# Gate and up of the second FFN, second half of the tokens: seven half-size products in place of eight

## The chip, the cores and the metric

The kernel runs on one core of one Trainium2 chip. The metric is the device time of one launch in microseconds; lower is better. All arithmetic is fp32: every factor of a matrix product is split into a high part of the type fp32r and the remainder, and a product is made of three matmuls (high by high, high by low, low by high).

## What is computed

One decoder layer for 1,024 prompt tokens and 64 sample tokens (1,088 in all, width 1,024). Around every sub-layer stands an RMSNorm before and one after:

```python
def swiglu(x, w_gu, w_down):
    gate, up = jnp.split(x @ w_gu, 2, axis=-1)
    return (jax.nn.silu(gate) * up) @ w_down

def macaron_half(x, g_pre, w_gu, w_down, g_post):
    return x + 0.5 * rmsnorm(swiglu(rmsnorm(x, g_pre), w_gu, w_down), g_post)
...
    hp = macaron_half(hp, ffn1_norm_pre[l], ffn1_w_gu[l], ffn1_w_down[l], ffn1_norm_post[l])
    ...
    hp = hp + rmsnorm(merge(fo, go, gg, gla_norm[l], w_out[l]), mix_norm_post[l])
    hp = macaron_half(hp, ffn2_norm_pre[l], ffn2_w_gu[l], ffn2_w_down[l], ffn2_norm_post[l])
```

Between the two FFNs lie attention and gated linear attention, which the change doesn't touch. The hidden width of an FFN is 2,752: 21 full blocks of 128 rows for gate and for up, and a tail of 64.

## The kernel before, in words

All activations lie transposed: 128 rows of the width on the partitions, tokens along the free axis. The second FFN runs twice, for tokens 0 to 511 (called f2 in the code, accumulator `p3.y`, in the trace and below `y0`) and for tokens 512 to 1,087 (called f3, 576 tokens, accumulator `p4.y`, the later `y1`). f3 is the last stage of the program. Its operand, the normed input of 576 tokens, lies split in `ub` (high and low); that of the first half lies in `ua`, which is free once f2 has made its last gate and up.

The hidden blocks are taken in groups: [0 (the tail), 1], [2 to 5], [6 to 9], [10 to 13], [14 to 17], [18, 19], [20, 21]. For a group, `job_gate` and `job_up` make gate and up of each block, and four jobs `job_down` then add the group's part of the down product to the accumulator. In f3 gate of one block is 24 matmuls on 256 tokens and 24 on 320 (eight blocks of the contraction by three), and up the same: 96 matmuls. ScalarE (ACT) takes Silu of gate out of PSUM, VectorE (DVE) multiplies it with up, and ACT and DVE split the result into `hh` and `hl`, the operands of the down product.

`Feed` brings the weights: a DMA of 512 KB into one of two buffers `wr`, a cast on ACT to `wh`, a subtraction on DVE to `wl`. There are three buffers each of `wh` and `wl`, so a weight is split only after the one three places earlier has been used up. The products go to three PSUM banks, `mm`; a bank is free when DVE or ACT has read it.

The program is written with a tile framework that tracks dependences by region and waits with semaphores. Each engine works through its own list strictly in order. The framework sorts these lists when it compiles, by its own model of what will be ready when, so an instruction can stand on an engine's list far from where the code issues it.

Of the kernel before, what the change touches and what calls it, by code (L numbers as in the profile page):

```python
# [8 lines left out]
F32 = mybir.dt.float32  # L9
# [23 lines left out]
NRAWW = 2  # L33
NCW = 320
# [31 lines left out]

class Feed:
# [7 lines left out]
    def _raw(self):  # L75
        s, nc = self.step, self.step.nc
        t = s.W.tile([P, KB * P], F32, name=s.uid("wr"), tag="wraw", bufs=NRAWW)
        pieces, _ = self.reqs[len(self.raws)]
        o = 0
        for p in pieces:  # L80
            n = p.shape[-1]
            nc.sync.dma_start(t[:, o:o + n], p)
            o += n
        self.raws.append((t, o))

    def _split(self):
# [5 lines left out]
        place = self.reqs[i][1]  # L92
# [8 lines left out]
    def pump(self, ahead=NW - 1):  # L101
        while len(self.parts) < min(len(self.reqs), self.freed + ahead):
            self._split()
        while len(self.raws) < min(len(self.reqs), len(self.parts) + NRAWW):
            self._raw()

# [6 lines left out]
    def free(self, n=1, ahead=NW - 1):  # L113
        self.freed += n
        self.pump(ahead)


class Step:
# [32 lines left out]
    def flush(self):  # L151
        while self.pend:
            self.pend.pop(0)()
# [142 lines left out]
    def norm(self, y, y0, c0, n, pool, post=None, pre=None, v=None, key=None):  # L296
# [24 lines left out]
        if post:  # L321
# [14 lines left out]
            if pre is None:  # L336
                return
# [17 lines left out]
    def ffn(self, w_gu, w_dn, f):  # L355
# [103 lines left out]
        def job_first(g, ws):  # L459
# [3 lines left out]
            for i, (c0, n) in enumerate(f.firsts):  # L463
                f.first(i)
                tail(ws[0], c0, n)
                if i == len(f.firsts) - 1:
                    self.feed.free(1, NW)
                gate(g[1], ws[1], c0, n)
# [12 lines left out]

        def job_down(g, d2, w, chunks, final):
            wt = None
            if HB_TAIL in g:
# [22 lines left out]
        for g, chunks, kind in f.plan:  # L507
# [5 lines left out]
            elif kind == "last":  # L513
# [4 lines left out]
                continue  # L518
            else:
# [9 lines left out]
    def work(self, jobs):  # L529
        self.feed = Feed(self, [r if isinstance(r, tuple) else (r, None) for rs, *_ in jobs for r in rs])  # L530
# [451 lines left out]


class Part:


    def __init__(self, **kw):
        self.__dict__.update(kw)


class StepB(StepA):
# [415 lines left out]
    def whole(self):  # L1407
# [122 lines left out]
        def mid4():  # L1530
# [5 lines left out]
        f2.after = lambda c0, n, v: self.norm(p3.y, 0, c0, n, p4.R, (5, self.h2, O["yT"]), None, v)  # L1536
# [8 lines left out]
                  plan=[(G[0], MID[1:], "first")] + [(g, MID[1:], "mid") for g in G[1:6]] + [(G[6], [(HALF, 320), (HALF + 320, 256)], "last")],  # L1545
                  place=lambda i: lambda: [u[:, 2 * i:2 * i + 2].rearrange("p a n -> p (a n)") for u in self.ua],
                  after=lambda c0, n, v: self.norm(p4.y, HALF, c0, n, p4.R, (5, self.h2, O["yT"]), None, v))

        f3.first = lambda i: self.need(("f2", CH[2 + i][0]))

        def start5():
            p4.close()
            f3.H, _ = self.pool("H2", keep=True)
        norm0 = self.norm(y, 0, *CH[0], F, pre=0, key="f1", v=[self.rms_quick(y, CH[0][1], F)])
# [100 lines left out]
```

## Time and profile before

| | |
|---|---|
| median of 3 runs | 2416.95 us (2416.03 to 2434.86) |
| profiled execution | 2429.76 us, of which 2428.0 us from its first to its last instruction |
| PE (TensorE) busy | 2346.4 us, 97% |
| DVE busy | 1174.9 us, 48% |
| ACT busy | 862.7 us, 36% |
| POOL (GpSimd) busy | 361.2 us, 15% |
| mean DMA rate | 136 GB/s |
| mean granted TensorE clock | 0.984 |

PE spans overlap: a matmul's record lasts longer than the distance to the next one, so the cost of a matmul is read from the distance of the starts. "PEld" is the weight load that goes beside the matmul before it. In f3 the trace has no POOL instruction from 2040 to 2340 us.

### The profile page before, as it was taken

The page shows a single profiled execution, that of the slowest core. Times are in us where ns is not written, and L with a number is a line of the kernel's source. Part 1 is how long each engine was busy: PE and PEld are TensorE (multiplying, and loading weights), DVE is VectorE, ACT ScalarE, POOL GpSimd, SP SyncE. Part 2 cuts the span into 40 slices and gives each one's busy share as a digit, 9 for nine tenths or more (in the row PEclk, how much of TensorE's full clock was granted, in tenths as well). Part 3 has the DMA queues.
Part 4 walks back from the last instruction along what each step waited for, and adds up shares of the span by engine and source line. Part 5 has one row for each costly group of instructions (what it writes and reads, how often), then busy time and mean ns, then how long its engine had stood idle before and what let it go on. Part 6 is the DMA issues. An engine that isn't in the chain of part 4 may idle for free.

```text
span 2428.0 us, 39284 instructions
## 1 busy us (share of the span) xinstructions
PE 2346.4 (97%) x15452; PEld 2074.3 (85%) x15452; DVE 1174.9 (48%) x2302; ACT 862.7 (36%) x1582; POOL 361.2 (15%) x420
## 2 busy tenths in 40 slices
PE   7999999999999999999998999999997999999997
PEld 6799999999989879899996656677787999999997
DVE  7223232232347774666464333358775774333345
ACT  5411111112134555755453222236455543222222
POOL 4000000000003230010134554611100320000002
PEclk9999999999999999999998999999998999999998
DMA  3111111111125476564357998755554534222222
GB/s 122 61 44 51 46 44 44 44 44 44 44 96 158 167 227 195 189 188 143 127 182 255 313 330 292 260 171 158 168 155 143 184 103 159 85 81 86 80 78 84
DMA packets 177082, 330.56 MB, mean 136 GB/s; under 512 B 25153, under 2 KB 100738, under 8 KB 176898
## 3 DMA queue, kind: packets, MB, share of 16 engines
q1 hardware_dynamic: 165234, 289.77, 36.8%
q0 software_dynamic: 11664, 38.28, 4.5%
q8 instruction: 122, 2.00, 0.3%
q14 instruction: 62, 0.51, 0.1%
HBM read 284.29 MB, written 43.69 MB: 135 GB/s over the span
## 4 chain that ended last, share of the span: by engine, by line
PE 76%; DVE 9%; DMA 4%; ACT 4%; issue 4%; POOL 2%; SPq 1%; POOLq 0%; DVEq 0%; ACTq 0%
PE mm L210 46%; PE mm L440 21%; PE po L878 2%; DVE wl L146 1%; PE sp L840 1%; DMA wr<-in_wout 1%; ACT wh L145 1%; PE tp L1073 1%; PE po L1088 1%; DVE qd L1177 1%; DVE fm L1060 1%; DVE pT L146 1%; PE pa L1218 1%; POOL y L328 1%; POOL ss L224 0%
## 5 line engine op out<-in xcount | busy, mean ns | idle before, releaser
L210 PE MATMUL mm<-ub,wh 128*128 128x320 f32 (+2 forms) x3776 | 774.9, 300 | 10.4 <-ACT ub L145 8.2
L210 PE MATMUL mm<-ua,wh 128*128 128x512 f32 (+2 forms) x2288 | 637.7, 365 | 2.2 <-ACT ua L351 1.4
L210 PEld LDWEIGHTS mm<-ub,wh 128*128 128x128 f32 (+1 forms) x3776 | 612.1, 190 | 19.4 <-ACT ub L145 8.4
L146 DVE TENSOR_TENSOR wl<-wr,wh 128x1024 fp32r<-128x1024 f32 (+1 forms) x294 | 356.5, 1213 | 448.3 <-ACT wh L145 445.3
L145 ACT CAST wh<-wr 128x1024 fp32r<-128x1024 f32 (+1 forms) x294 | 301.2, 1025 | 743.1 <-PE mm L210 314.7
L210 PE MATMUL mm<-ub,wl 128*128 128x320 f32 (+1 forms) x1872 | 556.1, 297 | 0.7 <-DVE wl L146 0.7
L210 PEld LDWEIGHTS mm<-ua,wh 128*128 128x128 f32 (+1 forms) x2288 | 401.2, 192 | 79.5 <-issue 23.9
L210 PE MATMUL mm<-ua,wl 128*128 128x512 f32 (+1 forms) x1136 | 406.3, 358 | 0.7 <-DVE wl L146 0.7
L210 PEld LDWEIGHTS mm<-ub,wl 128*128 128x128 f32 x1872 | 356.1, 190 | 0.9 <-DVE wl L146 0.9
L440 PE MATMUL mm<-hl,wh 128*128 128x256 f32 (+4 forms) x1088 | 353.1, 325 | 0.0
L440 PE MATMUL mm<-hh,wh 128*128 128x256 f32 (+2 forms) x1040 | 338.5, 326 | 1.4 <-DVE y L450 1.4
L440 PE MATMUL mm<-hh,wl 128*128 128x256 f32 (+2 forms) x1040 | 332.1, 320 | 0.0
L210 PEld LDWEIGHTS mm<-ua,wl 128*128 128x128 f32 x1136 | 217.2, 192 | 32.9 <-issue 1.6
L450 DVE TENSOR_TENSOR y<-y,mm 128x256 f32<-128x256 f32 (+2 forms) x272 | 130.3, 504 | 203.3 <-PE mm L440 202.9
L440 PEld LDWEIGHTS mm<-hl,wh 128*128 128x128 f32 (+1 forms) x1088 | 205.8, 189 | 21.1 <-issue 9.9
L224 POOL TENSOR_TENSOR ss<-ss,sq 128x256 f32<-128x256 f32 (+1 forms) x46 | 44.9, 977 | 1163.1 <-ACT sq L220 1162.5
L440 PEld LDWEIGHTS mm<-hh,wh 128*128 128x128 f32 x1040 | 196.1, 189 | 22.3 <-issue 9.1
L440 PEld LDWEIGHTS mm<-hh,wl 128*128 128x128 f32 x1040 | 196.4, 189 | 12.1 <-issue 0.4
L379 DVE TENSOR_TENSOR sg<-mm,sg 128x256 f32<-128x256 f32 (+4 forms) x112 | 55.8, 498 | 186.5 <-PE mm L210 184.4
L801 POOL DMA_INDIRECT pr<-in_cv,rows x128 | 127.5, 996 | 116.0 <-PE po L878 60.2
L145 ACT CAST hh<-sg 128x320 fp32r<-128x320 f32 (+2 forms) x128 | 62.5, 489 | 193.8 <-DVE sg L379 170.2
L373 ACT ACTIVATE sg<-mm 128x256 f32<-128x256 f32 (+4 forms) x112 | 49.1, 438 | 145.8 <-PE mm L210 145.7
(244 smaller groups left out, 2235.1 us busy)
## 6 DMA issues: line engine op xcount, KB each, us to landing
wr<-in_wgu SPq DMA_DIRECT2D x137, 512.0 KB
wr<-in_wd SPq DMA_DIRECT2D x60, 512.0 KB
pr<-in_ck SPq DMA_DIRECT2D x112, 256.0 KB
wr<-in_win SPq DMA_DIRECT2D x50, 512.0 KB
wr<-in_wout SPq DMA_DIRECT2D x32, 512.0 KB
h<-y SPq DMA_DIRECT2D x12, 512.0 KB
x<-h SPq DMA_DIRECT2D x24, 256.0 KB
wr<-in_wd SPq DMA_DIRECT2D x20, 256.0 KB
```

What stands on the lines that cost most here:

```text
L145: self.nc.scalar.copy(hi, src)
L146: self.nc.vector.tensor_tensor(out=lo, in0=src, in1=hi.bitcast(F32), op=ALU.subtract)
L210: nc.tensor.matmul(out, a, x[:, k, o:o + n], start=(k == 0 and j == 0), stop=(k == KB - 1 and j == len(ops) - 1))
L224: (nc.gpsimd if odd else nc.vector).tensor_tensor(out=s, in0=s, in1=sq[:, :n], op=ALU.add)
L328: (nc.gpsimd if k % 2 else nc.vector).tensor_tensor(out=rows(k), in0=rows(k), in1=xs[k // 2][:, k % 2, :n], op=ALU.add)
L373: nc.scalar.activation(out=t, in_=src, func=AF.Silu)
L379: nc.vector.tensor_tensor(out=out, in0=u, in1=t, op=ALU.mult)
L440: nc.tensor.matmul(pds[e], a, b, start=(i == 0 and j == 0), stop=(i == len(g) - 1 and j == len(ops) - 1))
L450: nc.vector.tensor_tensor(out=yk, in0=yk, in1=pds[e], op=ALU.add)
L801: nc.gpsimd.indirect_dma_start(out=raw[:, i], out_offset=None, in_=A["ck" if kind == "K" else "cv"].rearrange("g p n -> (g p) n"), in_offs ...
L840: nc.tensor.matmul(sp[32 * a:32 * a + 32, 256 * hf:256 * hf + 256], qz[p % 2][:, a, s, :], raw[:, :, a * P:(a + 1) * P], start=False, stop ...
L878: nc.tensor.matmul(po[r], pT[:, t, r], raw[:, :, a * P:(a + 1) * P], start=(t == 0), stop=False)
```

## The change

For blocks 2 to 19 (18 blocks, the five groups after the first) of f3, gate and up of a block are made by one level of Strassen's algorithm in its form with 15 sums. The two rows of the 2 by 2 weight matrix are gate and up of one block, its two columns the lower and the upper half of the contraction (512 each); the operand is cut into the same halves of the contraction and two halves of 288 tokens. There are seven products of 12 matmuls on 288 tokens, 84 matmuls per block.

- The weight sums are made per block on POOL. `Sums.load` loads four quarters of 256 KB (the tiles `wx`, `wz` and a part of `y0`) and makes three sums of 128x512, later a fourth. The weights to be split are then x, y, z of 1,024 columns and s4 of 512 (3.5 pieces where there were two). The old accumulator `y0` serves as room for y, s4 and three sums of the result.
- The operand sums (four of 4x288 columns, made in halves by `sevens` on DVE, split by ACT and DVE) go into `ua` and two new tiles `t4`.
- The results: ACT copies the first product, DVE makes seven additions of 288 columns, ACT takes Silu of 576 columns, POOL multiplies it with up, ACT and DVE split it.
- The fourth of seven products has a PSUM bank of its own, `mx`; the other six share the three banks `mm`.

The core of the diff:

```diff
+class Sums:
+    def load(self, s):
+        if self.first is self:
...
+            x, z = new("wx"), self.f.H.tile([P, 2 * h], F32, name=s.uid("wz"), tag="wz", bufs=2)
+            y, s4, a21 = self.f.old()
+            for t, src in ((a21, self.up[:, lo]), (z[:, hi], self.up[:, hi]), (x[:, lo], self.gate[:, lo]), (z[:, lo], self.gate[:, hi])):
+                nc.sync.dma_start(t, src)
+            for out, a, b, op in ((y[:, lo], a21, z[:, hi], ALU.add), (x[:, hi], y[:, lo], x[:, lo], ALU.subtract),
+                                  (y[:, hi], x[:, lo], a21, ALU.subtract)):
+                nc.gpsimd.tensor_tensor(out=out, in0=a, in1=b, op=op)
+            self.tiles = [(x, 2 * h), (y, 2 * h), (z, 2 * h), (s4, h)]
+        if self.i == 2:
...
+            s.nc.gpsimd.tensor_tensor(out=s4, in0=z[:, :h], in1=x[:, h:], op=ALU.subtract)
+        return self.first.tiles[self.i]
...
+        def seven(z, w, half, b, done):
...
+            z.turn = (z.turn + 1) % 4
+            ps = self.mm(n) if z.turn else self.px.tile([P, 512], F32, name=self.uid("mx"), tag="mx", bufs=1)[:, :n]
+            for k in range(KB // 2):
...
+                    nc.tensor.matmul(ps, a, x, start=(k == 0 and j == 0), stop=(k == KB // 2 - 1 and j == len(ops) - 1))
...
+            if i == 0:
...
+                seven(z, w, 0, "b11", lambda ps: nc.scalar.copy(z.q, ps))
+                seven(z, w, 1, "t2", lambda ps: add(z.u, z.q, ps))
+            elif i == 1:
+                seven(z, w, 1, "t3", lambda ps: add(z.v, z.u, ps))
+                def both(ps):
+                    add(z.u, z.u, ps)
+                    add(z.up[:, b], z.v, ps)
+                seven(z, w, 0, "t1", both)
+            elif i == 2:
+                seven(z, w, 0, "b21", lambda ps: add(sgs[hb][:, a], z.q, ps))
+                seven(z, w, 1, "t4", lambda ps: add(z.up[:, a], z.v, ps))
+            else:
...
+                def evac(ps):
+                    add(t[:, b], z.u, ps)
+                    nc.scalar.activation(out=t, in_=t, func=AF.Silu)
+                    nc.gpsimd.tensor_tensor(out=t, in0=t, in1=z.up, op=ALU.mult)
+                    self.soon(lambda: self.split(hh, hl, t))
+                seven(z, w, 0, "b22", evac)
...
+        def sevens():
...
+                for h in (slice(0, 2), slice(2, 4)):
+                    nc.vector.tensor_tensor(out=out[:, h], in0=p[:, h], in1=q[:, h], op=ALU.subtract)
...
+                    self.split(hi[:, h], lo[:, h], out[:, h])
...
-                  plan=[(G[0], MID[1:], "first")] + [(g, MID[1:], "mid") for g in G[1:6]] + ...
+                  plan=[(G[0], MID[1:], "first")] + [(g, MID[1:], "sevens") for g in G[1:6]] + ...
```

What stands on the engines' lists, at three places. Line numbers in these lists are those of the program that the list is of; a number behind a tile's name tells one tile of that name from another.

POOL, between the last norm of the first half (`y0<-y0,x`) and the end of the program. Before, the next instructions are the sums of squares (`ss`) of the last norm:

```order
L328 TENSOR_TENSOR y0_7664<-y0_7664,x_2886_20249 128x256
L328 TENSOR_TENSOR y0_7664<-y0_7664,x_2887_20251 128x256
L328 TENSOR_TENSOR y0_7664<-y0_7664,x_2888_20253 128x256
L224 TENSOR_TENSOR ss_3318_23960<-ss_3318_23960,sq_3322_23981 128x320
L224 TENSOR_TENSOR ss_3318_23960<-ss_3318_23960,sq_3326_24003 128x320
```

Now 90 instructions stand between them. A piece of these, from the first group of four (`wx_2951`, `wz_2952` are of block 4, `wx_2970`, `wz_2971` of block 5, `wx_3010`, `wz_3011` of block 6, which opens the next group; `sg_2953` is Silu of gate of block 3, `sg_2972` of block 4):

```order
L94 TENSOR_TENSOR y0_7664<-wz_2952_20619,wx_2951_20618 128x512
L89 TENSOR_TENSOR y0_7664<-y0_7664,wz_2971_20750 128x512
L89 TENSOR_TENSOR y0_7664<-wx_2970_20749,y0_7664 128x512
L89 TENSOR_TENSOR wx_2970_20749<-y0_7664,wx_2970_20749 128x512
L578 TENSOR_TENSOR sg_2953_20627<-sg_2953_20627,up_2954_20628 128x576
L94 TENSOR_TENSOR y0_7664<-wz_2971_20750,wx_2970_20749 128x512
L89 TENSOR_TENSOR y0_7664<-y0_7664,wz_3011_21010 128x512
L89 TENSOR_TENSOR y0_7664<-wx_3010_21009,y0_7664 128x512
L89 TENSOR_TENSOR wx_3010_21009<-y0_7664,wx_3010_21009 128x512
L578 TENSOR_TENSOR sg_2972_20758<-sg_2972_20758,up_2973_20759 128x576
```

So the multiplication of block 3 (L578, `sg_2953`) stands behind the three sums for the weights of block 5, that of block 4 behind those of block 6.

DVE, in a group of four. Before, the end of block 3 (`hl_2929` is its split result, in two pieces) with two weight splits among it:

```order
L146 TENSOR_TENSOR wl_2954_20692<-wr_2944_20574,wh_2953_20691 128x1024
L379 TENSOR_TENSOR sg_2945_20576<-mm_2951_20637,sg_2945_20576 128x256
L146 TENSOR_TENSOR hl_2929_20451<-sg_2945_20576,hh_2928_20450 128x256
L379 TENSOR_TENSOR sg_2945_20576<-mm_2952_20663,sg_2945_20576 128x320
L146 TENSOR_TENSOR wl_2960_20753<-wr_2950_20635,wh_2959_20752 128x1024
L146 TENSOR_TENSOR hl_2929_20451<-sg_2945_20576,hh_2928_20450 128x320
```

Now, from the sixth product of block 3 (`mm_2964`) to the fourth of block 4 (`mx_2979`). `wl_2969` is y of block 4, `wl_2977` is z of block 4, `wl_2981` is s4 of block 4, `hl_2929` the split result of block 3, `mm_2975` and `mm_2978` the second and third product of block 4:

```order
L551 TENSOR_TENSOR up_2954_20628<-y0_7664,mm_2964_20710 128x288
L192 TENSOR_TENSOR wl_2969_20746<-y0_7664,wh_2968_20745 128x1024
L551 TENSOR_TENSOR sg_2953_20627<-y0_7664,mm_2967_20729 128x288
L192 TENSOR_TENSOR wl_2977_20791<-wz_2952_20619,wh_2976_20790 128x1024
L192 TENSOR_TENSOR hl_2929_20491<-sg_2953_20627,hh_2928_20490 128x576
L551 TENSOR_TENSOR y0_7664<-y0_7664,mm_2975_20775 128x288
L192 TENSOR_TENSOR wl_2981_20824<-y0_7664,wh_2980_20823 128x512
L551 TENSOR_TENSOR y0_7664<-y0_7664,mm_2978_20794 128x288
L551 TENSOR_TENSOR y0_7664<-y0_7664,mx_2979_20807 128x288
L551 TENSOR_TENSOR up_2973_20759<-y0_7664,mx_2979_20807 128x288
```

The addition that reads `mm_2975`, and all behind it, now stand behind the split of block 3's result, which needs POOL's multiplication.

DVE, at the end of f2, where the last down products of the first half are added up (`y0<-y0,mm`). Before:

```order
L146 TENSOR_TENSOR wl_2811_19730<-wr_2802_19637,wh_2810_19729 128x1024
L377 SCALAR_TENSOR_TENSOR sg_2803_19639<-sg_2803_19639,mm_2809_19690 128x512
L146 TENSOR_TENSOR wl_2820_19797<-wr_2808_19688,wh_2819_19796 128x1024
L146 TENSOR_TENSOR hl_2755_19344<-sg_2803_19639,hh_2754_19343 128x512
L450 TENSOR_TENSOR y0_7664<-y0_7664,mm_2813_19735 128x256
L450 TENSOR_TENSOR y0_7664<-y0_7664,mm_2814_19748 128x256
L450 TENSOR_TENSOR y0_7664<-y0_7664,mm_2815_19764 128x256
L450 TENSOR_TENSOR y0_7664<-y0_7664,mm_2818_19780 128x256
L146 TENSOR_TENSOR wl_2831_19869<-wr_2812_19733,wh_2830_19868 128x1024
```

Now, with the first operand sums (L593) and their splits (`ua1`) among them:

```order
L192 TENSOR_TENSOR wl_2811_19730<-wr_2802_19637,wh_2810_19729 128x1024
L593 TENSOR_TENSOR y1_18685<-y1_18685 128x2x288 x3
L425 SCALAR_TENSOR_TENSOR sg_2803_19639<-sg_2803_19639,mm_2809_19690 128x512
L192 TENSOR_TENSOR wl_2820_19797<-wr_2808_19688,wh_2819_19796 128x1024
L192 TENSOR_TENSOR hl_2755_19344<-sg_2803_19639,hh_2754_19343 128x512
L192 TENSOR_TENSOR ua1_99<-y1_18685,ua0_98 128x576
L498 TENSOR_TENSOR y0_7664<-y0_7664,mm_2813_19735 128x256
L498 TENSOR_TENSOR y0_7664<-y0_7664,mm_2814_19748 128x256
L498 TENSOR_TENSOR y0_7664<-y0_7664,mm_2815_19764 128x256
L192 TENSOR_TENSOR ua1_99<-y1_18685,ua0_98 128x576 x2
L498 TENSOR_TENSOR y0_7664<-y0_7664,mm_2818_19780 128x256
L593 TENSOR_TENSOR y1_18685<-y1_18685 128x2x288
```

The code issues the operand sums with the first group of f3 (`sevens`), and the list has the first three of them ahead of the last multiplication by up of f2 (L425); all eight stand on DVE's list ahead of its first multiplication by up of f3.

More of the change, by code (lines that the diff above doesn't have):

```diff
@@ L33 @@
 NRAWW = 2
+NSUMS = 3
 NCW = 320
@@ L151, in flush @@
     def flush(self):
-        while self.pend:
-            self.pend.pop(0)()
+        pend, self.pend = self.pend, []
+        for fn in pend:
+            fn()
     def tick(self, us):
@@ L482, in job_down @@
         def job_down(g, d2, w, chunks, final):
             wt = None
+            if f.room and HB_TAIL in g:
+                self.need(("sevens", f.b0))
             if HB_TAIL in g:
```

92 lines of the change are left out of this document (84 added, 8 removed).

## The prediction

> **What bounds the kernel now.** I read the page first, then the stretches of the last stage, then PE's instructions in it one by one.
>
> ```profile
> PE 2346.4 (97%) x15452; PEld 2074.3 (85%) x15452; DVE 1174.9 (48%) x2302; ACT 862.7 (36%) x1582; POOL 361.2 (15%) x420
> PE 76%; DVE 9%; DMA 4%; ACT 4%; issue 4%; POOL 2%; SPq 1%; POOLq 0%; DVEq 0%; ACTq 0%
> 2040.00:2340.00 300.00, 300.00 (x2260) 300.00 (x2259) 111.09 (x172) 72.32 (x109) 0.00 (x0) 1.00 0.24 82
> 2030.56 0.40 PE L210 MATMUL mm<-ub,wh 128*128 128x256 f32 x2
> 2033.40 0.46 PE L210 MATMUL mm<-ub,wh 128*128 128x320 f32 x2
> 2036.93 0.40 PE L210 MATMUL mm<-ub,wh 128*128 128x256 f32 x2
> ```
>
> The first two lines are busy time by engine and the chain that ended last: PE carries both. The third is the stretch of 300 us in which nearly all of the changed work lies, its columns span, PE, weight load, DVE, ACT, POOL, clock, DMA share and GB/s. PE has no gap in it, the granted clock is 1.00, DVE works 111 us of 300, ACT 72, POOL nothing. So PE time saved here would be saved in full, as long as the others keep up. The last three lines are the starts of three runs of 24 matmuls: 2.84 us for 256 tokens (118.3 ns each), 3.53 us for 320 (147.1 ns). At 288, half way, a matmul takes 132.7 ns.
>
> **What PE saves.** A block had 96 matmuls of that mean, 12.74 us, and has 84, 11.15 us. 18 blocks lose 12 x 18 = 216 matmuls (PE's compiled list is shorter by just 216 rows), **28.7 us**.
>
> **What is added, and whether it hides.** The prices of the other engines:
>
> ```profile
> L146 DVE TENSOR_TENSOR wl<-wr,wh 128x1024 fp32r<-128x1024 f32 x47 | 57.6, 1225 | 92.0 <-ACT wh L145 92.0
> L145 ACT CAST wh<-wr 128x1024 fp32r<-128x1024 f32 x47 | 49.4, 1051 | 169.7 <-PE mm L210 85.7 <-PE mm L440 64.0 <-issue 20.0
> L450 DVE TENSOR_TENSOR y<-y,mm 128x320 f32<-128x320 f32 x32 | 14.9, 488 | 42.6 <-PE mm L440 42.6
> L450 DVE TENSOR_TENSOR y<-y,mm 128x256 f32<-128x256 f32 x32 | 12.5, 421 | 3.9 <-PE mm L440 3.9
> L146 DVE TENSOR_TENSOR wl<-wr,wh 128x512 fp32r<-128x512 f32 x16 | 11.7, 729 | 21.8 <-ACT wh L145 21.0 <-DMA k<-ks 0.7
> L146 DVE TENSOR_TENSOR hl<-sg,hh 128x512 fp32r<-128x512 f32 x40 | 27.5, 689 | 11.7 <-ACT hh L145 11.6
> L145 ACT CAST hh<-sg 128x512 fp32r<-128x512 f32 x40 | 24.7, 619 | 100.2 <-DVE sg L379 79.1 <-DVE sg L377 21.1
> L373 ACT ACTIVATE sg<-mm 128x512 f32<-128x512 f32 x20 | 11.9, 595 | 68.3 <-PE mm L210 68.3
> L1290 POOL TENSOR_TENSOR o<-o,gsq 128x512 f32<-128x512 f32 x8 | 10.7, 1336 | 79.9 <-DMA gsq<-ggs 68.5 <-DVE o L1287 11.5
> L1487 POOL COPY y<-o 128x512 f32<-128x512 f32 x4 | 2.4, 609 | 0.3
> L328 POOL TENSOR_TENSOR y<-y,x 128x256 f32<-128x256 f32 x36 | 34.0, 947 | 51.7 <-DVE y L327 42.5 <-DMA x<-h 4.5 <-DMA x<-in_xT 4.5
> ```
>
> An addition of 288 columns out of PSUM is half way between the two L450 rows, 0.455 us. Silu, cast and split of 576 columns are the 512 rows by 576/512: 0.67, 0.70 and 0.775. The new POOL sums of 512 columns have their like in L1290: 1.34 us (bounds: 0.61, the copy of that size, and 1.89, twice the 256 row); POOL's multiplication of 576 is 1.50.
>
> As a sum of busy time all fits. Per block DVE has 3 x 1.225 + 0.73 for the weights, seven additions (3.19) and 0.775, together 8.4 us; POOL 4 x 1.34 + 1.50 = 6.9 us; PE 11.15. But POOL and DVE don't run freely beside each other:
>
> ```profile
> 1230.24 0.86 POOL L328 TENSOR_TENSOR y<-y,x 128x256 f32<-128x256 f32 x1 [0.26 <-DVE y L327]
> 1231.36 2.66 POOL L328 TENSOR_TENSOR y<-y,x 128x256 f32<-128x256 f32 x1 [0.26 <-DVE y L327]
> 1231.54 1.22 DVE L146 TENSOR_TENSOR wl<-wr,wh 128x1024 fp32r<-128x1024 f32 x1
> 1235.57 0.98 POOL L328 TENSOR_TENSOR y<-y,x 128x256 f32<-128x256 f32 x1 [1.54 <-DMA x<-h]
> 1235.87 1.76 DVE L146 TENSOR_TENSOR wl<-wr,wh 128x1024 fp32r<-128x1024 f32 x1
> ```
>
> The same POOL addition takes 0.86 us alone and 2.66 beside DVE's weight split; the same split takes 1.22 or, begun while POOL works, 1.76, about the rest of POOL's addition more. One waits for the other to finish. I take it that a POOL sum and a weight split of DVE run one after the other, in turn. *SBUF — State Buffer* of the Trainium skill, section "Who interferes with whom", says just this: a DVE instruction with two SBUF inputs and a GpSimd instruction that reads SBUF share a port, and whichever comes second is blocked entirely. The trace agrees (2.66 for 0.86, 1.76 for 1.22); it speaks against this change, whose sums and weight splits are all of these two kinds.
>
> **The ring.** What decides is the order on the lists. POOL makes the three sums for block D (the next but one) ahead of the multiplication of block B. The first of them overwrites y, so it waits until y of block C is split; for that a weight buffer must be free, after B's sixth product. Behind the multiplication stand ACT's cast and DVE's split of B's result; behind these, on DVE, the addition that reads C's second product. The sixth product of C needs that PSUM bank. One turn, from that addition in one block to that in the next:
> - DVE: s4 split 0.73, three additions 1.37, x split 1.23, two additions 0.91, y split 1.23: 5.45 (their inputs are early by then; the cast of y waits for the sixth product, 1.59 us, and takes 1.05).
> - POOL: three sums 4.01 and the multiplication 1.50, with DVE's split of z, which goes in between, 1.23: 6.74. Silu is done by then.
> - ACT cast 0.70, DVE split 0.775, addition 0.455: 1.93. Four hand-overs between engines, 0.04 each by the starts and durations below (2071.79 + 0.42 to 2072.25): 0.16.
>
> ```profile
> 2071.79 0.42 DVE L379 TENSOR_TENSOR sg<-mm,sg 128x256 f32<-128x256 f32 x1 [0.68 <-PE mm L210]
> 2072.25 0.41 ACT L145 CAST hh<-sg 128x256 fp32r<-128x256 f32 x1 [2.06 <-DVE sg L379]
> ```
>
> The sum is **14.28 us** where PE has 11.15 us of work: PE waits 3.13 us per turn, more than the 1.59 us that a block saves. In a group of four there are two full turns. The first turn starts with DVE not yet late: from the sixth product's end y cast 1.05, y split 1.23, 6.74, 1.93 and six hand-overs (0.24), 11.19, against six products of 12 x 0.1327 = 1.59, 9.55: a wait of 1.64.
>
> At the end of a group the down products need the last block's result. From the last turn's addition: s4 split, three additions, first down weight's split, two additions, second down weight's split, addition (5.91), Silu 0.67, multiplication 1.50, cast 0.70, split 0.775, hand-overs 0.16: 9.72. PE has two products (3.18), 27 down matmuls of the other three blocks (18 x 0.118 + 9 x 0.147 = 3.45) and three that need only the cast (0.38): 7.0. A wait of 2.7. Before, the same place cost nothing, as the stretch without a gap shows.
>
> A group of four thus waits 1.64 + 2 x 3.13 + 2.7 = 10.6 us, four groups 42.4. The group of two has no sums ahead of its multiplications; from the sixth product of its second block cast 1.05, split 1.23, addition 0.455, Silu 0.67, 1.50, 0.70, 0.775 and 0.24 make 6.6 against 1.59 + 1.15 + 0.38 = 3.1 of PE: 3.5 us.
>
> **The operand sums.** They come where the first half's last down products are added up:
>
> ```profile
> 1963.00:1990.00 27.00, 27.00 (x224) 26.78 (x223) 18.57 (x34) 12.89 (x24) 3.78 (x4) 1.00 0.26 89
> ```
>
> DVE is busy 18.6 of 27.0 us there. Eight sums and eight splits of 576 columns at 0.775 add 12.4 us, 4.0 more than the stretch holds. PE waits for these additions to free its banks, so I take **4.0 us** (bounds 0, if they slide into other stretches, and 12.4, if all is in series).
>
> **Moved or added at nothing.** The weights' DMA carries the same bytes in quarters. A 512 KB load moves within some three slices of 0.75 us:
>
> ```profile
> GB/s 0 0 0 0 0 120 360 219 0 0 0 22 0 22 262 360 55 0 0 0 0 0 153 306 219 22 0 0 0 0 22 202 399 77 22 0 0 0 0 147
> ```
>
> The x quarter can start when x of the block before is split, some 6 us before POOL reads it in the ring: hidden, and a late one would lengthen the ring one for one. SP's list has the group's third and fourth down weights behind the quarters of a block that come some 6 us early, also hidden. The norm of the first half's output is pulled ahead of the first group's last split, 5 us of DVE under 17 us of down matmuls; after it come the first quarter (it overwrites `y0`, so it waits for the output's write), three POOL sums and a split, due when that down ends. I take nothing, with 5 us as the upper end. ACT's added casts (1.5 x 1.05 per block) lie beside PE.
>
> **The sum**: -28.7 + 42.4 + 3.5 + 4.0 = **+21.2 us**. The profiled execution, 2429.76 us (span 2428.0), would become 2451. It lies 12.8 above the median of the runs; on the median 2416.95 the forecast is **2438 us**, +0.9%.
>
> **Rivals.**
> 1. *No blocking between POOL and DVE.* For it: the split at 1231.54 took its 1.22 beside POOL; but there POOL was the one that waited. z's split leaves the ring: 13.05 a turn, waits 1.90 and, first, 0.41; a group 6.9, all 27.7 + 7.5 - 28.7 = +6.5: 2423. The row at 1235.87 is against it. This is also the time if the port rule of the Trainium skill's *SBUF — State Buffer* did not hold here, 15 us less.
> 2. *POOL is quick and the change pays.* At the copy's rate a sum is 0.61, the multiplication 0.69: the ring is 11.28, the first wait 0, the end 1.9, a group 2.2; with 2.7 for the pair and 4.0: 15.3 - 28.7 = -13.4: 2404. It decides at the point where a group waits (28.7 - 7.5)/4 = 5.3: per us on a sum a group's waits change by 3 x 4.125 + 1.125 = 13.5 us, so at 0.95 us a sum. Against it: every two-input row of POOL, 947 ns for half the columns.
> 3. *All hides* (the lists allow more than I see): 2388.
> 4. *POOL is slow.* 1.89 a sum, 2.13 the multiplication: a turn 16.6, a group 18.1, the pair 4.1: 80.6 - 28.7 = +52: 2469. For it: the 256 row with its 947; against it L1290. *Perfetto Trace Analysis* of the Trainium skill, section "GPSIMD Instruction", calls spans of this engine unreliable and advises the distance of consecutive starts; an L1290 sum at 1052.37 is followed by the next start at 1053.72 in the rows below, 1.35 us, and by that the sum stands.
>
> ```profile
> 1052.37 1.28 POOL L1290 TENSOR_TENSOR o<-o,gsq 128x512 f32<-128x512 f32 x1 [15.41 <-DMA gsq<-ggs]
> 1053.72 0.61 POOL L1487 COPY y<-o 128x512 f32<-128x512 f32 x1
> ```
>
> **Chances.** Forecast 0.45 (its own range 2427 to 2451), no blocking 0.15, POOL quick 0.13, all hides 0.07, POOL slow 0.20. The range, 2404 to 2460, leaves out the third rival and half of the fourth, 0.17. A measurement of this kernel tells about 1%, 24 us, from no change: faster by that only the third, 0.07; slower the fourth and the upper part of the forecast, 0.38; within it 0.55.
>
> **What would show it.** PE should show gaps of 2 to 3 us before each sixth product from the second block of a group on (ended by DVE's addition) and before the first down matmul on the last block's result (ended by ACT and DVE); a block in the middle of a group should take 14.3 us; POOL's multiplication should start 5 to 7 us after its Silu; DVE's z split should show 1.8 us and more. PE without gaps in the groups, or POOL sums under 0.95 us, would make it wrong.

## The result, and the profile after

The changed kernel takes 2455.93 us (median of 4 runs, 2447.20 to 2460.89), the kernel before 2421.24 us beside it on the same chip: a ratio of **1.0128, 95% interval 1.0096 to 1.0161**: 1.3% slower. The forecast was 2438 us, a ratio of 1.0087; the measured time lies above the forecast's own range (2427 to 2451) and within the whole one (2404 to 2460). The profiled execution has a span of 2457.8 us against 2428.0. A profile is of one execution, and executions of one kernel differ here by up to 22 us with their mean granted clock (in run 2 below, 2421.45 us at 0.986 and 2443.08 at 0.976), so a stretch read from a profile need not fit the ratio to the microsecond.

The first line is the page's busy time by engine, the second the stretch that the prediction read before (span, PE, weight load, DVE, ACT, POOL, clock, DMA share, GB/s), both of the changed kernel.

```profile
PE 2339.0 (95%) x15236; PEld 2058.8 (84%) x15236; DVE 1262.7 (51%) x2426; ACT 898.0 (37%) x1608; POOL 494.1 (20%) x510
2040.00:2340.00 300.00, 269.41 (x1913) 262.36 (x1912) 168.08 (x251) 95.25 (x122) 112.32 (x76) 0.97 0.24 79
```

PE has the 216 matmuls less, but where it was busy for 300.00 us of 300 it is now busy for 269.41: it stands idle for 30.6 us, more than the matmuls saved. And the clock, 1.00 before, is 0.97. DVE rose from 111 to 168 us, POOL from nothing to 112: neither is full.

Cutting PE's timeline where it goes from one kind of product to the next gives the length of each stage. The rows are whole stages: first of the kernel before (downs of the second group of four; first group's down), then of the changed kernel (first group's down; gate/up and downs of the second group of four).

```profile
2151.62:2177.22 25.60, 25.60 (x195) 25.60 (x193) 11.86 (x21) 4.56 (x5) 0.00 (x0) 1.00 0.24 83
2006.97:2024.19 17.22, 17.22 (x86) 12.54 (x85) 9.81 (x20) 9.91 (x22) 3.38 (x4) 1.00 0.79 249
```

```profile
2006.01:2032.44 26.43, 25.50 (x83) 18.14 (x82) 10.84 (x20) 9.62 (x22) 9.87 (x9) 0.63 0.61 190
2114.48:2164.37 49.89, 46.13 (x339) 44.83 (x337) 31.60 (x47) 19.84 (x26) 23.69 (x16) 1.00 0.23 78
2164.37:2195.94 31.57, 27.79 (x192) 27.15 (x193) 13.54 (x23) 5.46 (x6) 5.66 (x4) 0.95 0.26 79
```

| stage, us | before | after | measured | predicted |
|---|---|---|---|---|
| last downs of the first half (operand sums beside them) | 23.23 | 25.25 | +2.0 | +4.0 |
| first group, gate/up | 20.49 | 20.85 | +0.4 | 0 |
| first group, down | 17.22 | 26.43 | **+9.2** | 0 (upper end 5) |
| four groups, gate/up | 4 x 50.92 | 50.28, 49.89, 49.88, 49.88 | -3.8 | +6.1 |
| four groups, downs | 4 x 25.60 | 31.76, 31.57, 32.02, 32.16 | **+25.1** | +10.8 |
| pair, gate/up and downs | 39.58 | 39.50 | -0.1 | +0.3 |
| sum | 406.6 | 439.5 | **+32.9** | +21.2 |

The predicted gate/up of the four groups is 4 x 7.9 us of waits less 192 matmuls of 0.1327; that of the pair 3.5 us less 24.

The code ahead of this stretch is the same, but the stretch begins between 1953 and 1971 us in the profiles of this study. So below I compare its length, 406.6 us before and 439.5 after, and not spans.

**The ring is there.** PE's waits in the first group of four, from its timeline:

```profile
2052.95 0.53 PE L543 MATMUL mm<-t,wh 128*128 128x288 f32 x2 [0.85 <-DVE y L551]
2066.05 0.53 PE L543 MATMUL mm<-t,wh 128*128 128x288 f32 x2 [1.30 <-DVE y L551]
2079.15 0.53 PE L543 MATMUL mm<-t,wh 128*128 128x288 f32 x2 [1.30 <-DVE y L551]
2090.32 0.66 PE L488 MATMUL mm<-hh,wh 128*128 128x256 f32 x3 [3.89 <-ACT hh L191]
```

Three gaps ahead of sixth products, each ended by DVE's addition, and one ahead of the first down matmul on the last block's result. The turn is 2079.15 - 2066.05 = 13.10 us, 1.95 more than PE's 11.15; the gap in the row is smaller, since it is counted from the end of a record that outlasts the distance to the next start. One turn on POOL, on ACT (Silu, cast) and on DVE (z's split, the result's split, the addition that frees the bank):

```profile
2071.05 1.29 POOL L89 TENSOR_TENSOR y<-y,wz 128x512 f32<-128x512 f32 x1 [3.02 <-DVE wl L192]
2072.30 2.28 POOL L89 TENSOR_TENSOR y<-wx,y 128x512 f32<-128x512 f32 x1
2074.54 1.29 POOL L89 TENSOR_TENSOR wx<-y,wx 128x512 f32<-128x512 f32 x1
2075.79 1.44 POOL L578 TENSOR_TENSOR sg<-sg,up 128x576 f32<-128x576 f32 x1
2071.37 0.69 ACT L577 ACTIVATE sg<-sg 128x576 f32<-128x576 f32 x1 [0.92 <-DVE sg L551]
2077.27 0.67 ACT L191 CAST hh<-sg 128x576 fp32r<-128x576 f32 x1 [4.92 <-POOL sg L578]
2071.26 2.17 DVE L192 TENSOR_TENSOR wl<-wz,wh 128x1024 fp32r<-128x1024 f32 x1
2077.97 0.76 DVE L192 TENSOR_TENSOR hl<-sg,hh 128x576 fp32r<-128x576 f32 x1 [4.54 <-ACT hh L191]
2078.65 0.45 DVE L551 TENSOR_TENSOR y<-y,mm 128x288 f32<-128x288 f32 x1
```

Silu is done at 2072.06, and the multiplication starts 3.7 us later, behind three sums. The blocking shows on both sides: z's split takes 2.17 us instead of 1.23, the second sum 2.28 instead of 1.29. (The prediction read its row of 2.66 us for a POOL addition as beside one weight split. The split, from 1231.54 to the next start at 1232.67, is 1.13 of the 1.80 us above 0.86; two additions of DVE behind it, to the next start at 1233.35, come to the rest.)

**The group's end is worse than forecast, in two ways.** The first is on ACT, then POOL and SP, at the end of the same group:

```profile
2086.01 1.05 ACT L191 CAST wh<-wr 128x1024 fp32r<-128x1024 f32 x1 [4.05 <-DMA wr<-in_wd]
2086.96 0.68 ACT L577 ACTIVATE sg<-sg 128x576 f32<-128x576 f32 x1
2087.72 1.85 POOL L578 TENSOR_TENSOR sg<-sg,up 128x576 f32<-128x576 f32 x1 [6.58 <-ACT sg L577]
2082.24 15.80 SPq L117 DMA_DIRECT2D wr<-in_wd  x4
```

DVE's last addition (start 2084.00) ends at 2084.44, but Silu starts at 2086.96: ahead of it on ACT's list stands the cast of the group's third down weight. That weight's load goes out at 2082.24, when the split of the first down weight on DVE, itself late in the ring, gives its buffer back.

The second is the clock. These rows are stretches of 3.41 us, around the first group's down and around this group's end:

```profile
2005.95:2009.37 3.42, 3.42 (x18) 2.28 (x17) 3.42 (x10) 1.85 (x5) 1.70 (x2) 1.00 0.92 281
2009.37:2012.78 3.41, 2.72 (x13) 1.76 (x12) 3.16 (x8) 0.68 (x3) 2.70 (x2) 0.99 0.93 277
2012.78:2016.19 3.41, 3.18 (x10) 2.63 (x10) 0.00 (x0) 0.92 (x3) 0.00 (x0) 0.50 0.98 291
2029.85:2033.26 3.41, 3.41 (x12) 2.87 (x12) 2.13 (x2) 1.88 (x4) 1.20 (x1) 0.51 0.24 79
2033.26:2036.67 3.41, 3.41 (x28) 3.41 (x27) 1.53 (x2) 1.64 (x3) 2.32 (x3) 1.00 0.07 15
2087.87:2091.29 3.42, 0.83 (x4) 0.60 (x5) 1.20 (x2) 0.67 (x1) 1.70 (x1) 0.99 0.52 152
2091.29:2094.70 3.41, 3.41 (x15) 3.41 (x15) 1.33 (x3) 0.00 (x0) 0.00 (x0) 0.51 0.03 8
2094.70:2098.11 3.41, 3.41 (x29) 3.41 (x29) 1.83 (x3) 1.05 (x1) 0.00 (x0) 1.00 0.00 0
```

Behind the wait at the group's end the granted clock is 0.5 for one stretch, which costs about 3.41 x (1 - 0.54) = 1.6 us (0.54 is the columns that went through in it, at 118 ns for 256, over its length); behind the third and fourth group's wait it is two stretches. In the first group's down it falls at 2012.8 and stays at 0.5 for 20.5 us, six such stretches, until the dense products have begun. No wait there is longer than 0.46 us.

### The profile page after: what moved, and what is told of

It reads as the page before. It is cut to its first block, busy times and chain, and to the rows that moved or that the text cites. A ratio compares the mean times of both kernels' runs of the same rounds, so it can differ in the third digit from the quotient of the medians.

```text
span 2457.8 us, 39321 instructions
## 1 busy us (share of the span) xinstructions
PE 2339.0 (95%) x15236; PEld 2058.8 (84%) x15236; DVE 1262.7 (51%) x2426; ACT 898.0 (37%) x1608; POOL 494.1 (20%) x510
## 5 line engine op out<-in xcount | busy, mean ns | idle before, releaser
L257 PE MATMUL mm<-ub,wh 128*128 128x256 f32 (+2 forms) x2624 | 545.0, 303 | 10.6 <-ACT ub L191 8.0
L192 DVE TENSOR_TENSOR wl<-wr,wh 128x1024 fp32r<-128x1024 f32 (+1 forms) x258 | 311.9, 1209 | 351.3 <-ACT wh L191 349.7
L191 ACT CAST wh<-wr 128x1024 fp32r<-128x1024 f32 (+1 forms) x258 | 263.3, 1021 | 604.4 <-PE mm L257 220.7
L257 PEld LDWEIGHTS mm<-ub,wh 128*128 128x128 f32 (+1 forms) x2624 | 426.5, 191 | 19.7 <-ACT ub L191 8.2
L257 PE MATMUL mm<-ub,wl 128*128 128x256 f32 (+1 forms) x1296 | 386.2, 298 | 1.0 <-DVE wl L192 1.0
L488 PE MATMUL mm<-hl,wh 128*128 128x256 f32 (+4 forms) x1088 | 360.6, 332 | 0.4
L257 PEld LDWEIGHTS mm<-ub,wl 128*128 128x128 f32 x1296 | 247.7, 191 | 1.2 <-DVE wl L192 1.2
L488 PEld LDWEIGHTS mm<-hl,wh 128*128 128x128 f32 (+1 forms) x1088 | 211.5, 194 | 23.0 <-issue 10.8
L191 ACT CAST hh<-sg 128x512 fp32r<-128x512 f32 (+3 forms) x110 | 59.2, 538 | 226.1 <-DVE sg L427 133.0
L192 DVE TENSOR_TENSOR hl<-sg,hh 128x512 fp32r<-128x512 f32 (+3 forms) x110 | 65.2, 593 | 90.0 <-ACT hh L191 89.9
L427 DVE TENSOR_TENSOR sg<-mm,sg 128x256 f32<-128x256 f32 (+4 forms) x76 | 39.3, 517 | 133.7 <-PE mm L257 132.1
```

The lines of the kernel that those rows point to most:

```text
L191: self.nc.scalar.copy(hi, src)
L192: self.nc.vector.tensor_tensor(out=lo, in0=src, in1=hi.bitcast(F32), op=ALU.subtract)
L257: nc.tensor.matmul(out, a, x[:, k, o:o + n], start=(k == 0 and j == 0), stop=(k == KB - 1 and j == len(ops) - 1))
L427: nc.vector.tensor_tensor(out=out, in0=u, in1=t, op=ALU.mult)
L488: nc.tensor.matmul(pds[e], a, b, start=(i == 0 and j == 0), stop=(i == len(g) - 1 and j == len(ops) - 1))
```

## The experiments

Each ratio is against runs of the kernel before on the same chip. "Stretch" is the length that is 406.6 us before and 439.5 after. The rows of windows have the columns named above.

**1. The multiplication on DVE.** The kernel is the changed one but for

```diff
-                    nc.gpsimd.tensor_tensor(out=t, in0=t, in1=z.up, op=ALU.mult)
+                    nc.vector.tensor_tensor(out=t, in0=t, in1=z.up, op=ALU.mult)
```

> The changed kernel with the multiplication by up on DVE instead of POOL. If the ring runs through POOL's order (sums of the next block but one ahead of the multiplication), the gaps ahead of the sixth products go: gate/up of a group of four falls from 49.9 us to 44.6 to 46, and the wait at a group's end falls by about 1 us (0.78 instead of 1.85 for the multiplication); in all -20 to -26 us against the changed kernel, near 2432. If instead the weight splits and additions of DVE themselves set the pace (9 us of work a block, and now 0.7 more with two stops for Silu and the cast), gate/up of a group stays at 49 us or more and the time within 6 us of the changed kernel's.

Ratio 1.0010 (0.9994 to 1.0026), stretch 410.6 us. The second group's gate/up and downs, and z's split in that group:

```profile
2112.24:2156.93 44.69, 44.69 (x338) 44.69 (x337) 38.50 (x51) 20.18 (x26) 21.06 (x13) 1.00 0.27 89
2156.93:2187.04 30.11, 27.53 (x194) 27.00 (x193) 13.80 (x23) 5.45 (x6) 3.82 (x3) 0.94 0.27 80
2135.74 2.15 DVE L192 TENSOR_TENSOR wl<-wz,wh 128x1024 fp32r<-128x1024 f32 x1
```

PE is busy in all of 44.69 us: 336 x 133 ns, no wait left, as the first theory had it. z's split still takes 2.15 us, so the blocking alone does not make PE wait. The downs fell by only 1.5 us, and the stretch by 28.9, a little more than was expected.

**2. POOL's list in another order.** The multiplication stays on POOL, and the sums are put behind the one issued last (`s.mul`).

```diff
-                nc.gpsimd.tensor_tensor(out=out, in0=a, in1=b, op=op)
+                with ExitStack() as st:
+                    if s.mul is not None:
+                        st.enter_context(s.tc.issue_after(s.mul.ins))
+                    nc.gpsimd.tensor_tensor(out=out, in0=a, in1=b, op=op)
```

> The changed kernel with POOL's list in another order and nothing else: the multiplication of a block stands ahead of the three weight sums of the next block but one. Same work, same engines, and z's split on DVE still meets POOL. If the order of POOL's list made the ring, gate/up of a group falls from 49.9 to 44.6 to 46 us as with the multiplication on DVE, and only there: -16 to -21 us against the changed kernel, near 0.45% above before (ratio 1.003 to 1.006). If the lock of POOL and DVE alone, or POOL's 6.6 us of work a block, made it, gate/up stays at 48 us or more (ratio 1.010 or more).

Ratio 1.0041 (1.0018 to 1.0064), stretch 407.4 us. The profiled execution took 2424.53 us, the median is 2433.11: the stretch is that of one of the best executions. Second group's gate/up, the multiplication of one block in it, and the first group's down:

```profile
2097.58:2143.21 45.63, 45.17 (x338) 44.77 (x337) 31.94 (x48) 20.07 (x26) 18.32 (x12) 1.00 0.28 86
2122.64 1.63 POOL L583 TENSOR_TENSOR sg<-sg,up 128x576 f32<-128x576 f32 x1 [4.11 <-ACT sg L582]
2003.09:2021.60 18.51, 17.59 (x83) 12.33 (x82) 8.54 (x19) 8.94 (x21) 9.43 (x8) 1.00 0.84 258
```

Order alone takes 4.3 us from each group, on the same engines: the order of POOL's list made most of the ring's waits. The expectation was wrong in one point: z's split (1.21 us) no longer meets POOL here, so this run does not part order from blocking; the run before does. Not expected: the first group's down, in which nothing was changed and the two waits are still there, took 18.51 us at clock 1.00.

**3. ACT's casts of the down weights behind Silu**, the one issued last (`s.silu`).

```diff
-        s.split(hi[:, :n], lo[:, :n], t[:, :n])
+        with ExitStack() as st:
+            if s.silu is not None and not isinstance(req, Sums):
+                st.enter_context(s.tc.issue_after(s.silu.ins))
+            s.split(hi[:, :n], lo[:, :n], t[:, :n])
```

> The changed kernel with ACT's casts of a group's down weights from the second on put behind the Silu of the group's last block (on ACT's and DVE's lists; same work). If the third down weight, which comes late, holds Silu up, Silu starts 2 to 2.5 us sooner, the wait at a group's end falls from 3.6 to 3.9 us to 1.3 to 2 us, too short to bring the half clock, and the downs of a group fall from 31.8 to 27 to 28 us: -15 to -20 us against the changed kernel (ratio 1.005). If the multiplication on POOL and the chain behind it set the wait, it falls by under 1 us and the downs stay at 30.5 us or more (ratio 1.010 or more).

Ratio 1.0053 (1.0034 to 1.0073), stretch 422.2 us. The second group's downs, its Silu, and PE's wait for the result:

```profile
2153.26:2180.43 27.17, 26.26 (x193) 25.66 (x193) 13.70 (x23) 6.40 (x7) 5.24 (x4) 1.00 0.32 90
2153.88 0.69 ACT L582 ACTIVATE sg<-sg 128x576 f32<-128x576 f32 x1 [3.94 <-DVE sg L556]
2156.83 0.50 PE L493 MATMUL mm<-hh,wh 128*128 128x256 f32 x2 [0.45 <-ACT hh L196]
```

Silu starts 0.6 us after the downs begin; in the rows of the changed kernel above it was 4.2 (2086.96 against 2082.72). PE's wait falls from 3.64 to 0.45 us, the half clock does not come, and 31.57 becomes 27.17: -4.4 us in each group, with no work less. The cast that came too early was most of the group's end.

**4. The downs behind the next block's first two products.**

```diff
+                        jobs += held
+                        held = []
...
+            to = held if kind == "sevens" and len(g) == 4 else jobs
             for d2 in range(4):
-                jobs.append(([[w_dn[d2][:, 2 * P * g[0]:2 * P * (g[-1] + 1)]]], ...
+                to.append(([[w_dn[d2][:, 2 * P * g[0]:2 * P * (g[-1] + 1)]]], ...
```

The first two lines stand behind the place where a block's job goes on the list, so that the downs follow the first job of the next group. The edit also moves `make(g)`, the making of the group's result tiles, from the first job of a group to its fourth, which now stands behind the downs of the group before.

> The changed kernel with the first two products of the next group's first block ahead of each group's down products (four places). If the last block's result is what PE waits for there, 3.2 us of products and another order of ACT's casts cover the 3.6 to 3.9 us, and with the wait the stretch of slow matmuls behind it goes too: downs of a group back from 31.8 us to about 25.7, -22 to -25 us in all, near 2433. If the slow matmuls come from what runs beside them (weights, DMA, sums) and not from the wait, only the idle time goes and each group's downs still take 27.5 us or more: -14 to -16.

```profile
2167.01:2193.06 26.05, 26.05 (x195) 25.65 (x193) 12.05 (x21) 4.88 (x5) 4.69 (x4) 1.00 0.33 106
```

Ratio 1.0036 (1.0022 to 1.0051), stretch 418.4 us, -21.1. Wait and half clock went together, as the first theory had it.

**5. An artificial wait in the kernel before.** In each of five groups the first product of a block waits for a chain of m = 2, 4, 8, 12 and 1 copies on ACT.

```diff
+            t = f.H.tile([P, 512], F32, name=self.uid("st"), tag="st", bufs=1)
+            for i in range(m):
+                nc.scalar.copy(t[:, :320], t[:, :320] if i else self.past)
+            self.ahead = self.mm(n)
+            nc.tensor.matmul(self.ahead[:, :2], t[:, :P], self.ones[:, :2], start=True, stop=True)
```

> The kernel before with an artificial wait in each of five groups of the second half: PE's next product waits for a chain of 2, 4, 8, 12 and 1 copies on ACT (about 1, 1.7, 3.5, 5 and 0.6 us). If a wait alone halves the granted clock behind it, the matmuls after the two long ones run at 220 ns (256) and 270 ns (320) apart for some 4 us, against 118 and 147 ns, and those after the short ones do not: a loss of about 2 us beyond each long wait. If the half clock needs something else of the changed kernel, the spacing is 118 and 147 ns behind all five.

This kernel ran once, so there is a profile and no ratio. The waits came out at 1.84, 2.83, 5.01, 6.97 and 0.93 us. Stretches of 3.41 us around the first three:

```profile
2045.61:2049.02 3.41, 2.54 (x21) 2.55 (x22) 2.12 (x3) 1.24 (x3) 0.00 (x0) 1.00 0.29 80
2124.11:2127.53 3.42, 1.17 (x9) 1.18 (x10) 2.12 (x3) 2.46 (x6) 0.00 (x0) 0.99 0.21 53
2127.53:2130.94 3.41, 3.41 (x18) 3.41 (x17) 0.00 (x0) 0.00 (x0) 0.00 (x0) 0.51 0.26 101
2130.94:2134.35 3.41, 3.41 (x26) 3.41 (x25) 0.00 (x0) 0.38 (x1) 0.00 (x0) 1.00 0.00 0
2209.45:2212.86 3.41, 2.97 (x14) 2.97 (x15) 0.00 (x0) 0.39 (x1) 0.00 (x0) 0.50 0.14 56
2212.86:2216.27 3.41, 3.41 (x17) 3.41 (x17) 0.00 (x0) 0.38 (x1) 0.00 (x0) 0.51 0.02 5
```

A wait alone does it; nothing else of the changed kernel is needed. 0.93 and 1.84 us cost only about 0.5 us beyond themselves, at full clock; 2.83, 5.01 and 6.97 us cost 2.0, 3.3 and 2.6 us more. The clock changes only on one grid: 2127.5, 2130.9, 2209.4, 2216.3, 2294.8 and 2301.6 lie whole multiples of 3.413 us apart. What goes with it is the share of full-speed columns in the window before, counted from the rows at 118 ns for 256 columns (one matmul is 0.03 to 0.04 of a window, so the count is no finer). From 1950 us on, in all profiles, windows with 0.40 or less are followed by half clock, those with 0.46 or more by full clock. Between the two both happen: 0.43 was followed by half clock in the changed kernel (from 2009.3) and by full clock in run 2 (from 2006.2), 0.45 in run 1 (from 2016.6) by half clock. A window at half clock that is busy throughout reaches about 0.5, enough to come back. Where a wait lies on the grid matters too. At the end of run 2's fourth group a wait of 2.56 us was shared out over these two windows, which hold 0.41 and 0.48, and the clock stayed whole:

```profile
2296.35:2299.76 3.41, 1.53 (x11) 1.27 (x10) 1.23 (x1) 1.45 (x3) 1.93 (x2) 1.00 0.56 157
2299.76:2303.17 3.41, 2.24 (x13) 1.76 (x14) 2.15 (x4) 0.63 (x1) 3.41 (x3) 1.00 0.17 65
```

At the end of its second group a wait of 2.10 us fell into one window, left 0.27 in it, and brought half clock.

*TensorE: Matmul & The Clock Gate* of the Trainium skill, section "Part 1: The HAM clock gate", describes a free-running window of 3413 ns and two states; the grid agrees. The rule of the Trainium skill in that page's section "HAM oscillation", no idle gaps over some 3.4 us, is too mild for this case: 2.83 us was enough here, 2.10 us in run 2 and 1.51 us in run 8.

**6. The pulled-forward norm alone**, in the kernel before, with no sums and no Strassen products; `early` is set at the end of the first group's gate/up.

```diff
+        if self.step.early:
+            self.step.early = False
+            self.step.need(("o", CH[1][0]))
```

> The kernel before, with one part of the change alone: the norm of the first half's output is pulled ahead of the first group's weight splits, as in the changed kernel; no sums, no Strassen products. If the 9.2 us in the first group's down come from this order (two short waits and then half the clock), the down takes about 26 us here too, and the kernel is 8 to 10 us slower than before. If they come from the operand sums, the quarters or POOL's sums, which are not in this kernel, the down takes 17 to 18 us and the time is that of before.

Ratio 1.0035 (1.0013 to 1.0057), stretch 409.5 us; the first group's down takes 19.81 us. Three stretches in it:

```profile
2016.23:2019.65 3.42, 2.50 (x11) 1.52 (x11) 2.08 (x5) 0.74 (x2) 1.85 (x1) 1.00 0.97 304
2019.65:2023.06 3.41, 3.41 (x12) 2.80 (x13) 0.91 (x2) 1.70 (x4) 0.00 (x0) 0.50 0.83 278
2023.06:2026.47 3.41, 3.41 (x17) 2.23 (x16) 0.08 (x1) 1.46 (x4) 0.00 (x0) 1.00 0.76 251
```

Between the two theories in this profile: the order of the norm brings the half clock by itself, but for one window. The window at half speed holds 0.44 here and the clock comes back; in the changed kernel the window there holds 0.38, and the next ones 0.34 to 0.41. The profiled execution took 2437.18 us and the median of eight is 2442.62, 7.3 above the kernel before: over all executions the loss is nearer to the first theory's 8 to 10 us than to the 2.6 us of this stage. In 16 of this stage's 80 matmuls 64 rows are active, and around these the starts at 256 columns are 0.31 us apart where others are 0.12 (the kernel before, from 2007 us). So at full clock the stage runs at 0.53 to 0.7, at half clock at 0.34 to 0.41, for six windows too little to come back.

**7. The last hl ahead of the norm**, in the changed kernel, at the end of the first group's gate/up.

```diff
                 up(g[1], ws[2], c0, n)
+            if f.room:
+                self.flush()
```

> The changed kernel with one edit alone: the split of the first group's last hl stands ahead of the second half of the pulled-forward norm on DVE. If the two waits of 0.46 us in the first group's down, which the split's lateness brings, tip the clock there, its 80 matmuls take 17.2 to 18.5 us at clock 1.00 instead of 26.4, and nothing else changes: about -9 us, ratio 1.008 to 1.010. If the half clock there has another cause (the sums on POOL, DMA), the down stays at 25 us or more.

```profile
2007.71:2025.29 17.58, 17.03 (x83) 12.11 (x81) 7.96 (x19) 8.57 (x21) 9.47 (x8) 1.00 0.78 238
```

17.58 us at clock 1.00; ratio 1.0094 (1.0071 to 1.0116), stretch 432.5 us. That is 7.0 us less where the stage alone gives 8.85: each other stage is within 0.7 us of what it was, but the groups of four are a little longer together, with a new wait of 0.56 us at the first product behind the down. The two waits of 0.46 us are gone. With the windows laid anywhere over this stage the lowest share is 0.53; with the changed kernel's order, in run 2's profile, it is 0.35, and whether a window falls there differs from execution to execution. Four profiles with that order had the long half clock (the changed kernel and runs 1, 3 and 4), run 2 did not. But its window from 2006.2 holds 0.43, as the one that tipped the clock in the changed kernel does, so what decides at this edge stays open.

**8. All three cures**: the edits of runs 1, 4 and 7 together.

> The changed kernel with three edits: the multiplication on DVE, the group's down products behind the next block's first two products, and the split of the first group's last hl ahead of the norm that was pulled forward (the stage of each is read apart). If the three causes are independent, gate/up of a group takes 44.7 us, the downs 25.6 to 26, and the first group's down falls from 26.4 back to 17.2 to 18 at a full clock, since the two waits that tipped it go: 20 to 23 us faster than before (ratio 0.991). If the norm's 4 us on DVE push another late (the weight splits behind it), the first group's down stays at half clock near 25 us and the ratio is 0.995 or more.

Ratio **0.9931** (0.9911 to 0.9951), stretch 386.1 us. First group's down, then the second group's gate/up and downs:

```profile
2003.70:2021.08 17.38, 17.03 (x84) 12.12 (x82) 7.96 (x19) 8.56 (x21) 9.48 (x8) 1.00 0.80 244
2095.48:2140.17 44.69, 44.69 (x339) 44.69 (x337) 39.88 (x52) 20.87 (x28) 21.08 (x13) 1.00 0.27 84
2140.17:2165.78 25.61, 25.61 (x194) 25.60 (x193) 12.06 (x21) 4.77 (x5) 3.81 (x3) 1.00 0.34 103
```

The three stages are within 0.2 us of what they would be without any wait, and the stretch is 20.5 us shorter than before.

**9. The same with the multiplication on POOL**: the edits of runs 2, 4 and 7.

> The changed kernel with the multiplication left on POOL but ahead of the sums on its list, the down products behind the next block's first two products, and the last hl ahead of the norm. If POOL's order, the group's end and the first group's clock are the whole loss, the stages are 44.7 (gate/up), 25.6 to 26 (downs) and 17.2 to 18 us (first down), and the kernel is 20 to 23 us faster than before (ratio 0.991), as with the multiplication on DVE. If DVE was what the multiplication's move to DVE left at its limit, this one is the faster of the two by some us; if POOL's lock costs more than DVE's added work, the slower.

```profile
2099.01:2145.29 46.28, 45.41 (x339) 44.81 (x337) 33.67 (x48) 20.54 (x27) 25.08 (x17) 1.00 0.25 77
```

Ratio 0.9953 (0.9935 to 0.9970), stretch 394.4 us: better than before, but 1.6 us a group behind DVE's version. POOL's sums of a block now end late, the cast of x waits for them (3.53 us at 2139.09), and behind it DVE's additions free PE's banks late.

**10. Run 8 with the pair's casts behind Silu**, the edit of run 3 for weights of 512 columns alone.

```diff
+            if s.silu is not None and n == 4 * P and not isinstance(req, Sums):
```

> The fastest version so far (multiplication on DVE, down products behind the next block's first two, hl ahead of the norm) with one more edit: in the group of two, ACT's second and third down-weight casts stand behind Silu, and DVE's splits of them behind the multiplication. The wait there should fall from 2.10 to about 1 us, too short for a half-clock window behind it, and the group's downs from 18.0 to 15 to 15.5 us: 2.5 to 3 us less, ratio 0.992 against 0.993. If the second down weight comes late in its place, PE waits for that instead and the downs stay above 17 us.

```profile
2330.98:2347.78 16.80, 14.29 (x99) 12.92 (x97) 12.06 (x23) 5.01 (x7) 0.00 (x0) 1.00 0.35 113
```

Ratio **0.9921** (0.9902 to 0.9940), stretch 385.8 us. The pair's downs fall from 17.96 to 16.80 us, less than expected, and not by shorter waits: PE's waits in the stage are 2.5 us, in run 8 they are 2.2, and the longest is 1.61 for 1.51. What went is one window of half clock, and the likely reason is where the grid lay: at the worst place a window over this stage would hold 0.23 here and 0.33 in run 8, so another execution may have the half clock again. Runs 8 and 10 can't be told apart; both beat both kernels.

## Why the prediction came out as it did

The direction and the mechanism were right: PE waits where it was said to, released by the instructions that were named, and the waits outweigh 28.7 us of matmuls. The matmuls' part was right as well: 133 ns at 288 columns, and 44.69 us for a group without waits. The sum, +21.2 for a measured +32.9 in the stretch, missed by terms that partly cancel: the group's ends and the first down came out 23.5 us too small, the ring and the rest about 12 too large. So the size is in part luck.

- **The ring, too large.** 14.28 us a turn, measured 13.10. DVE's leg to POOL's start took 5.50 us for 5.90 (with its first addition), POOL's 6.22 for 6.74, the rest 1.38 for 1.64. On DVE the durations in the rows overlap: additions of 0.45 us start 0.36 apart, splits of 1.23 are followed after 1.14. On POOL the sums follow 1.25 us apart where 1.34 was taken, and z's split holds the second one up for 0.99 us, not 1.23. The waits of a group came to 49.89 - 44.69 = 5.2 us and not 7.9. POOL's price (1.34, measured 1.29) and the blocking (z's split 2.17 of 1.23) held. All four rivals fall by these rows: the blocking is there, a sum takes 1.29 us and not 0.95 or 1.89, and PE does wait. How much of a turn the blocking costs was not tried by itself: without the second sum's 0.99 us it would be 12.11, still above 11.15.
- **The group's end, too small**: 2.7 us forecast, 6.0 to 6.6 measured. The step that failed is "the group's third and fourth down weights ... also hidden". The quarters ahead of them were indeed early, but the third weight also waits for its buffer, and its cast stands ahead of Silu on ACT's list, which the prediction did not look at for this place. Run 3 gives 4.4 of the 6.0 us to it, 1.6 of that through the clock.
- **The first group's down**: "I take nothing, with 5 us as the upper end", measured +9.2. The pulled-forward norm was seen, the two waits it makes were in the bound, and they are 0.92 us. What was not seen is that two short waits in a stage of low use can halve the clock for most of the stage. No row of the kernel before showed a half clock in this part.
- **The operand sums** 4.0 us, measured 2.0; the pair 3.5, measured 3.05.
- What should show it: gaps of 2 to 3 us were 0.85 to 1.30; the multiplication 5 to 7 us after its Silu was 3.7 after Silu's end and 4.4 after its start.

## What to carry to other kernels

A saving on the full engine is worth only what the lists of the others let through: with POOL 20% and DVE 51% busy, three places in their lists (sums ahead of a multiplication, a cast ahead of Silu, a norm ahead of a split) turned -28.7 into +32.9 us, and putting three pieces of work elsewhere made the same arithmetic 0.7 to 0.8% faster than before. For each instruction that PE waits for, read what stands ahead of it on its own engine and whether that waits for a DMA. Where PE's waits come to half of any 3.4 us, or a stage runs at little more than half of full columns, price the half clock behind it as well as the wait, and look at more than one execution: whether it comes depended on the place of the windows.

## What was not expected of the hardware

- The granted clock changes from window to window of 3.413 us and goes with the share of full-speed columns in the last one: 0.40 and less gave half clock, 0.46 and more full clock, and between them both occurred. A wait of 2.83 us cost 2.0 us more behind it; one of 1.84 us, 0.5.
- A stage that runs at 0.53 to 0.7 at full clock runs at 0.34 to 0.41 at half clock and stayed there for six windows: two waits of 0.46 us and what followed cost 8.85 us (26.43 against 17.58), in four profiles with that order, and not in run 2's.
- Back to back, DVE's instructions start about 0.08 us sooner than their durations say, and POOL's sums follow 1.25 us apart for 1.29. This is part of why a turn of 14.3 us worked out from durations was 13.1.
